# The down projection of a fp32 feed-forward layer, emitted in an explicit order per engine

## The chip, the cores and the metric

The kernel runs on one core of a Trainium2 chip. The metric is the device time of one execution in microseconds (us). A core has a matmul engine (TensorE, PE in the profile), a vector engine (VectorE, DVE), an activation engine (ScalarE, ACT), a general engine (GpSimd, POOL) and SyncE (SP), which here only issues DMAs. Each engine runs its own instruction queue in order and waits on semaphores for what others produce.

## The reference

One decoder layer over a sequence of 2048 tokens of width 1024: a mixer of three kinds of heads, then a gated feed-forward block with a short causal convolution. The change lies in the feed-forward block:

```python
def _conv_glu(h, w_up, conv_w, conv_b, w_down):
    u = _causal_dwconv(h @ w_up, conv_w) + conv_b
    gate, up = jnp.split(u, 2, axis=-1)
    return (jax.nn.silu(gate) * up) @ w_down
...
    x = x + _mixer(...)
    h = _rms(x, norm_ffn_g[l])
    x = x + _conv_glu(h, w_up[l], ffn_conv_w[l], ffn_conv_b[l], w_down[l])
```

Everything is float32. `w_up` is 1024 x 5632, `w_down` 2816 x 1024.

## The kernel before, in words

**Number format.** Matmul operands are split in two parts, a high part rounded to the fast fp32r format and the remainder `lo = x - h`. A product is the sum of three matmuls: high-high, high-low, low-high. So each operand tile costs a ScalarE copy (`h`) and a subtraction on VectorE or GpSimd (`lo`) before TensorE can read it.

**Halves.** The feed-forward block runs over the sequence in two halves (`hf` 0 and 1, 1024 tokens each): `ffn_up(0)`, `ffn_down(0)`, `ffn_up(1)`, `ffn_down(1)`. `ffn_up` writes the gated activations, in seven combinations, to the scratch tensor `s_g` in DRAM (lines L1112 and L1119, DMAs on ScalarE's queue), and `w_blocks` writes four combinations of blocks of `w_down` to `s_w`, in half 0 only.

**Down projection.** `ffn_down` multiplies 2 x 2 blocks by the Strassen-Winograd scheme: seven products instead of eight. A product (inner function `product`, matmuls at L1187) has `nj` = 11 steps j; a step takes one 128 x 512 tile of `s_g` (`g_parts`: load L1151 on SyncE's queue, copy L1152 on ScalarE, subtraction L1153 on VectorE) and one of the weights (`w_parts`: load L1160 from `s_w` or L1165 from `w_down`, copy L1166 on ScalarE, subtraction L1167 on GpSimd), and issues 3 matmuls for each of four 128 x 512 output tiles. The four output tiles of a product are two PSUM tiles of two banks; `ps_tile` rotates over four such places. The products run in the order of pairs (operand of `s_g`, operand of the weights) (0,4), (1,5), (5,1), (6,2), (3,3), (4,0), (2,6).

**Sums and stores.** After a product VectorE adds it into an accumulator (`u`, `v`; helper `tt`, L1205) or into the output. Four quarters of the output of a half leave: after products 2, 5, 6 and 7. For each, `base` loads the residual x2 (four tiles of tag `tmp`, four buffers, L1210, SyncE's queue) at step j = 4 of the product, and `store` adds and sends it out (L1218, DMA on ScalarE's queue). The first quarter's x2 is loaded straight into an accumulator (L1202). ScalarE copies the first product to `u` (L1224).

**Next half's operands.** `h_parts(k, 1, 0)` and `h_parts(k, 1, 1)` prepare the right operands of `ffn_up(1)` in half 0: at step 4 of the second and of the fourth product they emit, for four blocks dt one after the other, loads of `s_h` (L957), differences (VectorE, L962) and splits (`h_split`: ScalarE L944, VectorE or GpSimd L945). `up_blocks(k, k.hpool, 0, "a11 a12 a22")` at step 4 of the last product loads (L988) and splits (L993 on ScalarE, L994 on GpSimd) the first three weight blocks of `ffn_up(1)`.

**Buffers.** Operand tiles of the down projection come from one pool of 23 buffers of 128 x 512 (`fw`, tag `w`), which `ffn_up` also uses for its weight blocks; accumulators from 5 buffers (tag `u`), x2 tiles from 4 (tag `tmp`). `hpool` has 10 buffers. A tile's buffer is free once every reader of the previous tile in it is done.

**What sets the order.** The program is written with a framework whose planner simulates the engines and places each instruction in its engine's queue when its simulated inputs and buffers are ready, earlier emitted ones first. So the order of each queue around the down projection is the planner's: it may place loads, splits and sums of a product, the next half's operands and the up projection's matmuls (L1030) among each other. The queues then run in that order on the chip, each instruction waiting for its semaphores. All buffer waits and dependencies are put in by the framework.

Of the kernel before, what the change touches and what calls it, by code (L numbers as in the profile page):

```python
# [9 lines left out]
F32 = mybir.dt.float32  # L10
F32R = mybir.dt.float32r
# [3 lines left out]
AF = mybir.ActivationFunctionType  # L15
ALU = mybir.AluOpType
# [4 lines left out]
P = 128  # L21
# [8 lines left out]
NP = DFF // P  # L30
BLK = 512
# [9 lines left out]
RZ, RA = 2.5, 2  # L41

ZC = 6

ORDER = (
    "bo ci cg bv b0 b1 c0 c1 k0 k1 q0 q1 v0 v1",
# [895 lines left out]
def h_split(k, n, dt, x, eng):  # L942
    h, lo = k.hp[n]
    k.nc.scalar.activation(h[:, dt, :], x, AF.Copy)  # L944
    eng.tensor_tensor(lo[:, dt, :], x, h[:, dt, :].bitcast(F32), op=ALU.subtract)  # L945


def h_parts(k, hf, part):

    nc = k.nc  # L950
    for dt in range(4):
        def tmp():
            return k.t(k.hpool, [P, BLK], tag="w")

        def raw(q, s):
            t = tmp()
            nc.sync.dma_start(t, k.s_h[hf, q, s, :, dt, :])  # L957
            return t

        def sub(x, y):  # L960
            t = tmp()
            nc.vector.tensor_tensor(t, x, y, op=ALU.subtract)  # L962
            return t

        r12, r22 = raw(0, 1), raw(1, 1)
        if part == 0:
            r11, r21 = raw(0, 0), raw(1, 0)
            h_split(k, "b11", dt, r11, nc.gpsimd)
            t1 = sub(r12, r11)
            t2 = sub(r22, t1)  # L970
            h_split(k, "t1", dt, t1, nc.vector)
            h_split(k, "t2", dt, t2, nc.vector)
            h_split(k, "b21", dt, r21, nc.gpsimd)
            h_split(k, "t4", dt, sub(t2, r21), nc.vector)
        else:
            h_split(k, "t3", dt, sub(r22, r12), nc.vector)
            h_split(k, "b22", dt, r22, nc.gpsimd)


def up_blocks(k, fw, p, names):  # L980


    nc = k.nc

    def raw(q, ct):
        t = k.t(fw, [P, 4, P], tag="w")
        src = k.a["w_up"][0][q * BLK : (q + 1) * BLK, ct * P : (ct + 1) * P]
        nc.sync.dma_start(t, src.rearrange("(dt p) c -> p dt c", p=P))  # L988
        return t

    def parts(t):
        h, lo = (k.t(fw, [P, 4, P], F32R, tag="w") for _ in range(2))
        nc.scalar.activation(h, t, AF.Copy)  # L993
# [10 lines left out]
    if "s1" not in names:  # L1004
        for n, q, ct in (("a11", 0, p), ("a12", 1, p), ("a22", 1, NP + p)):
            if n in names:
                blocks[n] = parts(raw(q, ct))
        return blocks
# [92 lines left out]
def ps_tile(k, shape):  # L1101

    k.psp = k.psp[1:] + k.psp[:1]
    return k.t(k.psp[-1], shape, tag="ps")
# [31 lines left out]
def ffn_down(k, hf, fw):  # L1136

    nc = k.nc  # L1140
    first = {}
    x2_at = k.s_x2[hf * HALF : (hf + 1) * HALF].rearrange("(s i p) c -> p s i c", p=P, i=4)
    out_at = k.out[0, hf * HALF : (hf + 1) * HALF].rearrange("(s i p) c -> p s i c", p=P, i=4)

    def quarter(x, s, n):
        return x[:, s, :, n * BLK : (n + 1) * BLK]

    def g_parts(n, j):
        h, lo = (k.t(fw, [P, BLK], F32R, tag="w") for _ in range(2))
        raw = lo.bitcast(F32)  # L1150
        nc.sync.dma_start(raw, k.s_g[hf, n, j])  # L1151
        nc.scalar.activation(h, raw, AF.Copy)  # L1152
        nc.vector.tensor_tensor(lo, raw, h.bitcast(F32), op=ALU.subtract)  # L1153
        return h, lo

    def w_parts(n, j):
        h, lo = (k.t(fw, [P, BLK], F32R, tag="w") for _ in range(2))
        if n < 4:
            raw = lo.bitcast(F32)
            nc.sync.dma_start(raw, k.s_w[n, j])  # L1160
        else:
            raw = k.t(fw, [P, BLK], tag="w")
            q, c = ((0, 0), (1, 0), (1, 1))[n - 4]
            r = (q * (NP // 2) + j) * P
            nc.sync.dma_start(raw, k.a["w_down"][0][r : r + P, c * BLK : (c + 1) * BLK])  # L1165
        nc.scalar.activation(h, raw, AF.Copy)  # L1166
        nc.gpsimd.tensor_tensor(lo, raw, h.bitcast(F32), op=ALU.subtract)  # L1167
        return h, lo

    def product(na, nb, mid=None, last=False):  # L1170

        ps = [ps_tile(k, [P, 2, BLK]) for _ in range(2)]
        tiles = [ps[i // 2][:, i % 2, :] for i in range(4)]
        nj = NP // 2

        tail = 3 if last else 1
        parts = []
        for j in range(nj):
            parts.append((g_parts(na, j), w_parts(nb, j)))
            if mid is not None and j == 4:  # L1180
                mid()
            js = [j] if j < nj - tail else list(range(nj - tail, nj)) if j == nj - 1 else []
            for i in range(4):
                for m in js:
                    g, w = parts[m]
                    for c, (x, y) in enumerate(((0, 0), (0, 1), (1, 0))):
                        nc.tensor.matmul(  # L1187
                            tiles[i],
                            g[x][:, i * P : (i + 1) * P],
                            w[y],  # L1190
                            start=m == 0 and c == 0,
                            stop=m == nj - 1 and c == 2,
                        )
        return tiles

    def acc():
        t = [k.t(fw, [P, 2, BLK], tag="u", bufs=5) for _ in range(2)]
        return [t[i // 2][:, i % 2, :] for i in range(4)], t

    def load(t, s, n):  # L1200
        for i in range(2):
            nc.sync.dma_start(t[i], quarter(x2_at, s, n)[:, 2 * i : 2 * i + 2, :])  # L1202

    def tt(o, x, y, op=ALU.add):
        nc.vector.tensor_tensor(o, x, y, op=op)  # L1205

    def base(xs, s, n):
        for i in range(4):
            x = k.t(fw, [P, BLK], tag="tmp", bufs=4)
            nc.sync.dma_start(x, quarter(x2_at, s, n)[:, i, :])  # L1210
            xs.append(x)

    def store(xs, v, ps, s, n, op):

        for i in range(4):
            tt(ps[i], v[i], ps[i], op)
            tt(xs[i], xs[i], ps[i])
            nc.scalar.dma_start(quarter(out_at, s, n)[:, i, :], xs[i])  # L1218

    v, vt = acc()  # L1220
    p1 = product(0, 4, lambda: load(vt, 0, 0))
    u, _ = acc()
    for i in range(4):
        nc.scalar.activation(u[i], p1[i], AF.Copy)  # L1224
        tt(v[i], v[i], p1[i])
    p2 = product(1, 5, (lambda: h_parts(k, 1, 0)) if hf == 0 else None)
    for i in range(4):
        tt(v[i], v[i], p2[i])
    for i in range(2):
        nc.scalar.dma_start(quarter(out_at, 0, 0)[:, 2 * i : 2 * i + 2, :], vt[i])  # L1230
    p6 = product(5, 1)
    for i in range(4):
        tt(u[i], u[i], p6[i])
    p7 = product(6, 2, (lambda: h_parts(k, 1, 1)) if hf == 0 else None)
    v, _ = acc()
    for i in range(4):
        tt(v[i], u[i], p7[i])
    x4, x5, x3 = [], [], []
    p4 = product(3, 3, lambda: base(x4, 1, 0))
    store(x4, v, p4, 1, 0, ALU.subtract)  # L1240
    p5 = product(4, 0, lambda: base(x5, 1, 1))
    for i in range(4):
        tt(u[i], u[i], p5[i])
    store(x5, v, p5, 1, 1, ALU.add)

    def mid():
        base(x3, 0, 1)
        if hf == 0:
            first.update(up_blocks(k, k.hpool, 0, "a11 a12 a22"))

    p3 = product(2, 6, mid, last=hf == 1)
    store(x3, u, p3, 0, 1, ALU.add)
    return first


# [18 lines left out]
def _trunk(ctx, tc, a, out):  # L1274
    nc = tc.nc
    k = K(ctx, tc, a, out)
# [32 lines left out]
    with ExitStack() as ms:  # L1309
# [29 lines left out]
        with ExitStack() as at:  # L1339
# [14 lines left out]
            w = w_out_load(k, pool(wo, "wo", 1, side="right"), pool(wor, "wor", 1, side="right"))  # L1354
# [173 lines left out]
```

## Time and profile before

| | us |
|---|---|
| median of 3 runs | 3068.32 (3062.26 to 3069.09) |
| the profiled execution | 3064.58 |
| its span, first to last instruction | 3062.8 |
| mean granted TensorE clock | 0.965 of full |
| down projection, half 0: first to last matmul of L1187 | about 2120.8 to 2396.3 |
| down projection, half 1 | about 2823.1 to 3056.4 |

The profile comes from one execution. Its page lists busy times by engine, the span in 40 slices (busy tenths, granted clock, DMA), the DMA queues, the chain that ended last, and groups of instructions by source line with the idle time in front of them and what ended that. The trace behind it answers questions on single instructions, on waits (who waited for whom), and on stretches of time. In rows of the timeline a bracket `[idle before <-releaser]` tells how long the engine stood idle before the instruction and what released it; `x15` is the number of instructions merged into the row. PE is the matmul, PEld the weight load that goes with it; SPq and ACTq are instructions that only the queue of that engine carries, such as the issue of a DMA. A few per cent of the matmul records are missing.

### The profile page before, as it was taken

The numbers are of one execution on the slowest core, as the hardware profiler recorded it, in microseconds if no ns is written. First come the engines' busy times: TensorE is split into PE (matmuls) and PEld (weight loads), VectorE is DVE, ScalarE is ACT, GpSimd is POOL, SyncE is SP. The second block draws the span as 40 slices with busy tenths as digits, with TensorE's granted clock in tenths as the row PEclk, the third lists the DMA queues.
The fourth block names the chain that finished last, engine by engine and source line by source line (L and its number), as shares of the span: only waits on it lengthen the run. The fifth ranks groups of instructions, "written<-read, shape, count | busy, mean of one in ns | idle before, by whom it ended". The sixth has DMA issues, their size and how long they took to land. (4 is left out here: it accounts for less than half of the span.)

```text
span 3062.8 us, 43239 instructions
## 1 busy us (share of the span) xinstructions
PE 2867.9 (94%) x15181; PEld 2356.9 (77%) x15181; DVE 2029.6 (66%) x3637; ACT 1267.4 (41%) x2138; POOL 1419.4 (46%) x1149
## 2 busy tenths in 40 slices
PE   7999999899888988999999999999698999999998
PEld 7889999898765665666787788888487788888776
DVE  6427688757388877777546677776743677777534
ACT  3232432313144556776324444444442444444433
POOL 2133434633255656656202666665653544443533
PEclk9999999999988989999999999999799999999998
DMA  5333434423443034450356444546665333334654
GB/s 165 117 120 125 145 101 139 137 69 113 126 94 95 23 75 105 90 101 15 117 178 208 136 163 159 160 160 203 217 210 184 122 105 104 104 104 152 220 180 171
DMA packets 331897, 406.88 MB, mean 133 GB/s; under 512 B 30882, under 2 KB 219376, under 8 KB 328512
## 3 DMA queue, kind: packets, MB, share of 16 engines
q1 hardware_dynamic: 291520, 326.98, 35.8%
q10 hardware_dynamic: 37808, 68.76, 6.1%
q0 software_dynamic: 2352, 8.39, 1.0%
q8 instruction: 119, 1.95, 0.3%
q14 instruction: 98, 0.80, 0.1%
HBM read 276.05 MB, written 127.98 MB: 132 GB/s over the span
## 5 line engine op out<-in xcount | busy, mean ns | idle before, releaser
L994 POOL TENSOR_TENSOR w<-w,w 128x512 fp32r<-128x512 f32 x308 | 416.9, 1367 | 399.4 <-ACT w L993 291.4
L1187 PE MATMUL ps<-w,w 128*128 128x512 f32 x1848 | 453.5, 406 | 51.0 <-ACT w L1166 31.9
L1187 PEld LDWEIGHTS ps<-w,w 128*128 128x128 f32 x1848 | 358.1, 196 | 145.5 <-ACT w L1166 40.0
L164 PE MATMUL w<-whi,hhi 128*128 128x256 f32 (+1 forms) x1280 | 367.5, 288 | 2.3 <-DVE pg L226 1.7
L164 PE MATMUL w<-wlo,hhi 128*128 128x256 f32 (+1 forms) x1280 | 366.0, 287 | 0.6 <-POOL wlo L155 0.6
L164 PE MATMUL w<-whi,hlo 128*128 128x256 f32 (+1 forms) x1280 | 365.1, 286 | 0.0
L1167 POOL TENSOR_TENSOR w<-w,w 128x512 fp32r<-128x512 f32 x154 | 220.9, 1443 | 274.9 <-ACT w L1166 233.6
L781 POOL TENSOR_TENSOR pl<-pf,ph 128x512 fp32r<-128x512 f32 (+1 forms) x224 | 268.3, 1210 | 172.3 <-ACT ph L778 111.2
L993 ACT ACTIVATE w<-w 128x512 fp32r<-128x512 f32 x308 | 184.6, 628 | 273.3 <-POOL w L994 78.2
L1153 DVE TENSOR_TENSOR w<-w,w 128x512 fp32r<-128x512 f32 x154 | 158.2, 1048 | 147.9 <-ACT w L1152 142.7
L164 PEld LDWEIGHTS w<-whi,hhi 128*128 128x128 f32 x1280 | 244.0, 191 | 3.9 <-issue 2.2
L164 PEld LDWEIGHTS w<-wlo,hhi 128*128 128x128 f32 x1280 | 243.6, 191 | 1.8 <-POOL wlo L155 1.0
L164 PEld LDWEIGHTS w<-whi,hlo 128*128 128x128 f32 x1280 | 243.6, 191 | 0.2
L743 DVE TENSOR_REDUCE mx<-m 128x1 f32<-128x512 f32 (+2 forms) x320 | 188.6, 605 | 63.8 <-PE m L738 33.6
L776 ACT ACTIVATE pf<-s 128x512 f32<-128x512 f32 (+1 forms) x320 | 168.5, 539 | 140.2 <-DVE pl L781 49.3
L155 POOL TENSOR_TENSOR wlo<-wraw,whi 128x1024 fp32r<-128x1024 f32 (+1 forms) x56 | 137.8, 2481 | 171.9 <-ACT whi L154 169.0
L778 ACT ACTIVATE ph<-pf 128x512 fp32r<-128x512 f32 (+1 forms) x320 | 178.1, 575 | 46.1 <-PE pv L796 39.0
L999 DVE TENSOR_TENSOR w<-w,w 128x512 f32<-128x512 f32 x176 | 151.2, 878 | 69.1 <-DMA w<-in_w_up_dram 61.1
L1152 ACT ACTIVATE w<-w 128x512 fp32r<-128x512 f32 x154 | 97.0, 630 | 192.6 <-DMA w<-s_g 112.3
L1045 DVE SCALAR_TENSOR_TENSOR u<-ps,fcol,u 128x1023 f32<-128x1023 f32 x88 | 108.9, 1279 | 90.7 <-ACT u L1044 90.7
L769 PE MATMUL s<-QB,KB 70*128 70x512 f32 (+1 forms) x320 | 133.4, 417 | 29.3 <-ACT pf L776 29.0
L738 PE MATMUL m<-KB,QB 70*128 70x512 f32 (+2 forms) x320 | 135.3, 438 | 26.4 <-DVE mx L743 13.5
(345 smaller groups left out, 7087.6 us busy)
## 6 DMA issues: line engine op xcount, KB each, us to landing
w<-in_w_up_dram SPq DMA_DIRECT2D x182, 256.0 KB
w<-s_g SPq DMA_DIRECT2D x154, 256.0 KB
w<-in_w_down_dram SPq DMA_DIRECT2D x110, 256.0 KB
wraw<-in_w_in_dram SPq DMA_DIRECT2D x48, 512.0 KB
s_g<-u ACTq DMA_DIRECT2D x88, 256.0 KB
w<-s_w SPq DMA_DIRECT2D x88, 256.0 KB
s_g<-w ACTq DMA_DIRECT2D x66, 256.0 KB
w<-s_h SPq DMA_DIRECT2D x48, 256.0 KB
```

Of the source, the lines that this page charges most:

```text
L155: nc.gpsimd.tensor_tensor(lo[:, q : q + n, :], raw, h.bitcast(F32), op=ALU.subtract)
L164: nc.tensor.matmul(out, lsl(lhs[a], i), rsl(rhs[b], i), start=(i == 0 and j == 0), stop=(i == n - 1 and j == 2))
L743: nc.vector.tensor_reduce(mx[:, i, kb : kb + 1], ps[:, 0:n], axis=AX.X, op=ALU.max)
L776: nc.scalar.activation(pf[:, c0:], ps[:, c0:], AF.Exp)
L778: nc.scalar.activation(ph[:, c0:], pf[:, c0:], AF.Copy)
L781: eng.tensor_tensor(pl[:, c0:], pf[:, c0:], ph[:, c0:].bitcast(F32), op=ALU.subtract)
L993: nc.scalar.activation(h, t, AF.Copy)
L994: nc.gpsimd.tensor_tensor(lo, t, h.bitcast(F32), op=ALU.subtract)
L999: nc.vector.tensor_tensor(t, x, y, op=op)
L1153: nc.vector.tensor_tensor(lo, raw, h.bitcast(F32), op=ALU.subtract)
L1167: nc.gpsimd.tensor_tensor(lo, raw, h.bitcast(F32), op=ALU.subtract)
L1187: nc.tensor.matmul(tiles[i], g[x][:, i * P : (i + 1) * P], w[y], start=m == 0 and c == 0, stop=m == nj - 1 and c == 2,)
```

## The change

All of `ffn_down` is put in a region in which every engine keeps the order in which instructions are emitted (`manual_schedule`). Where the region's instructions fall among instructions outside it is still the planner's. The 7 x 11 = 77 steps are numbered through, and the loop emits for step i, in this order:

- the loads of step i + 4 (`AHEAD`);
- at j = 7 of the products 1, 5, 6, 7, the loads of the four x2 tiles (for the first product into `tmp` tiles too, not into an accumulator);
- at j = 1 to 4, the store of one output tile of the product before, on SyncE's queue instead of ScalarE's;
- in half 0, at steps 8, 15, ... 57, the loads of one of eight pieces of the next half's operands (`h_unit`), and at step 65 those of its first weight blocks (`up_first`); their splits follow five steps later;
- the splits of step i + 2;
- the matmuls of step i (in half 1 the last three steps of the last product tile by tile, as before);
- at j = 0 to 3, the sum of one output tile of the product before.

The matmuls, the number of VectorE sums, the bytes moved and the buffers are as before; 512 KB loads and stores of x2 and of the first quarter become 256 KB ones. `up_first` also serves the first half, ahead of `ffn_up(0)`; there it issues its three loads before its splits.

```diff
-def h_parts(k, hf, part):
-    nc = k.nc
-    for dt in range(4):
...
+def h_unit(k, hf, part, dt):
...
+    r12, r22 = raw(0, 1), raw(1, 1)
+    if part == 0:
+        r11, r21 = raw(0, 0), raw(1, 0)
+
+    def rest():
         if part == 0:
-            r11, r21 = raw(0, 0), raw(1, 0)
             h_split(k, "b11", dt, r11, nc.gpsimd)
             t1 = sub(r12, r11)
             t2 = sub(r22, t1)
...
+    return rest
+
+def up_first(k):
+    raws = {}
+    for n, q, ct in (("a11", 0, 0), ("a12", 1, 0), ("a22", 1, NP)):
+        t = raws[n] = k.t(k.hpool, [P, 4, P], tag="w")
...
+        nc.sync.dma_start(t, src.rearrange("(dt p) c -> p dt c", p=P))
+    def rest():
+        blocks = {}
+        for n, t in raws.items():
+            h, lo = blocks[n] = tuple(k.t(k.hpool, [P, 4, P], F32R, tag="w") for _ in range(2))
+            nc.scalar.activation(h, t, AF.Copy)
+            nc.gpsimd.tensor_tensor(lo, t, h.bitcast(F32), op=ALU.subtract)
+        return blocks
+    return rest
...
+    def loads(i):
+        n, j = steps[i]
+        raws[i] = load_g(prods[n][0], j), load_w(prods[n][1], j)
+
+    def parts(i):
+        (gr, gh, gl), (wr, wh, wl) = raws.pop(i)
+        nc.scalar.activation(gh, gr, AF.Copy)
+        nc.scalar.activation(wh, wr, AF.Copy)
+        nc.vector.tensor_tensor(gl, gr, gh.bitcast(F32), op=ALU.subtract)
+        nc.gpsimd.tensor_tensor(wl, wr, wh.bitcast(F32), op=ALU.subtract)
+        ready[i] = (gh, gl), (wh, wl)
...
+    def x2_tile(s, n, i):
+        t = k.t(fw, [P, BLK], tag="tmp", bufs=4)
+        nc.sync.dma_start(t, quarter(x2_at, s, n)[:, i, :])
+        return t
...
+    def sums(n, i, ps):
+        if n == 0:
+            nc.scalar.activation(st["u"][i], ps, AF.Copy)
+            tt(st["c"][i], st["u"][i], st["x"][i])
+        elif n == 1:
+            tt(st["x1"][i], st["c"][i], ps)
...
+        if n in (4, 5, 6):
+            x = st["x"][i]
+            tt(ps, st["u" if n == 6 else "v"][i], ps, ALU.subtract if n == 4 else ALU.add)
+            tt(x, x, ps)
+    def store(n, i):
+        if n in where:
+            nc.sync.dma_start(quarter(out_at, *where[n])[:, i, :], st["x1" if n == 1 else "x"][i])
+    side = {}
+    if hf == 0:
+        for m in range(8):
+            side[8 + 7 * m] = lambda m=m: h_unit(k, 1, m // 4, m % 4)
+        side[65] = lambda: up_first(k)
+    later = {}
+    tail = 3 if hf == 1 else 1
+    with k.tc.manual_schedule():
+        for i in range(AHEAD):
+            loads(i)
+        for i in range(2):
+            parts(i)
+        tiles = {}
+        for i, (n, j) in enumerate(steps):
+            if i + AHEAD < len(steps):
+                loads(i + AHEAD)
+            if j == 7 and n in (0, 4, 5, 6):
+                st["x"] = [x2_tile(*(where[n] if n else (0, 0)), t) for t in range(4)]
+            if n > 0 and 1 <= j <= 4:
+                store(n - 1, j - 1)
+            if i in side:
+                later[i + 5] = side[i]()
+            if i + 2 < len(steps):
+                parts(i + 2)
+            if i in later:
+                first = later.pop(i)() or first
+            if j == 0:
+                tiles[n] = quads([ps_tile(k, [P, 2, BLK]) for _ in range(2)])
...
+                for t in range(4):
+                    mm(tiles[n], i, t)
+            if n > 0 and j < 4:
...
+                sums(n - 1, j, tiles[n - 1][j])
+    for t in range(4):
+        sums(6, t, tiles[6][t])
+        store(6, t)
     return first
...
-    first = up_blocks(k, k.hpool, 0, "a11 a12 a22")
+    first = up_first(k)()
```

More of the change, by code (lines that the diff above doesn't have):

```diff
@@ L43 @@
 ZC = 6
+AHEAD = 4
 ORDER = (
@@ L945, in h_split, with tmp, raw, sub @@
     eng.tensor_tensor(lo[:, dt, :], x, h[:, dt, :].bitcast(F32), op=ALU.subtract)
-def h_parts(k, hf, part):
+def h_unit(k, hf, part, dt):
     nc = k.nc
-    for dt in range(4):
[L952 to L965, printed above, removed]
+    def tmp():
+        return k.t(k.hpool, [P, BLK], tag="w")
+    def raw(q, s):
+        t = tmp()
+        nc.sync.dma_start(t, k.s_h[hf, q, s, :, dt, :])
+        return t
+    def sub(x, y):
+        t = tmp()
+        nc.vector.tensor_tensor(t, x, y, op=ALU.subtract)
+        return t
+    r12, r22 = raw(0, 1), raw(1, 1)
+    if part == 0:
+        r11, r21 = raw(0, 0), raw(1, 0)
+    def rest():
         if part == 0:
-            r11, r21 = raw(0, 0), raw(1, 0)
             h_split(k, "b11", dt, r11, nc.gpsimd)
@@ L977, in h_parts @@
             h_split(k, "b22", dt, r22, nc.gpsimd)
+    return rest
+def h_parts(k, hf, part):
+    for dt in range(4):
+        h_unit(k, hf, part, dt)()
+def up_first(k):
+    nc = k.nc
+    raws = {}
+    for n, q, ct in (("a11", 0, 0), ("a12", 1, 0), ("a22", 1, NP)):
+        t = raws[n] = k.t(k.hpool, [P, 4, P], tag="w")
+        src = k.a["w_up"][0][q * BLK : (q + 1) * BLK, ct * P : (ct + 1) * P]
+        nc.sync.dma_start(t, src.rearrange("(dt p) c -> p dt c", p=P))
[7 more added lines that the diff above has]
+    return rest
 def up_blocks(k, fw, p, names):
@@ L1003, in up_blocks @@
     blocks = {}
[L1004 to L1008, printed above, removed]
     a11, a21, a22, a12 = raw(0, p), raw(0, NP + p), raw(1, NP + p), raw(1, p)
@@ L1146, in quarter, with load_g @@
         return x[:, s, :, n * BLK : (n + 1) * BLK]
-    def g_parts(n, j):
+    def load_g(n, j):
         h, lo = (k.t(fw, [P, BLK], F32R, tag="w") for _ in range(2))
@@ L1151, in g_parts, with load_w @@
         nc.sync.dma_start(raw, k.s_g[hf, n, j])
[L1152 to L1156, printed above, removed]
+        return raw, h, lo
+    def load_w(n, j):
         h, lo = (k.t(fw, [P, BLK], F32R, tag="w") for _ in range(2))
@@ L1163, in w_parts @@
             q, c = ((0, 0), (1, 0), (1, 1))[n - 4]
-            r = (q * (NP // 2) + j) * P
+            r = (q * nj + j) * P
             nc.sync.dma_start(raw, k.a["w_down"][0][r : r + P, c * BLK : (c + 1) * BLK])
[L1166 to L1194, printed above, removed]
@@ L1196, in acc @@
-    def acc():
[L1197 to L1202, printed above, removed]
+        return raw, h, lo
+    nj = NP // 2
+    prods = ((0, 4), (1, 5), (5, 1), (6, 2), (3, 3), (4, 0), (2, 6))
+    steps = [(n, j) for n in range(7) for j in range(nj)]
+    raws, ready = {}, {}
+    def loads(i):
+        n, j = steps[i]
+        raws[i] = load_g(prods[n][0], j), load_w(prods[n][1], j)
@@ new lines, in parts, with mm @@
+    def parts(i):
[5 more added lines that the diff above has]
+        ready[i] = (gh, gl), (wh, wl)
+    def mm(tiles, i, tile):
+        n, j = steps[i]
+        g, w = ready[i]
+        for c, (x, y) in enumerate(((0, 0), (0, 1), (1, 0))):
+            nc.tensor.matmul(
+                tiles[tile],
+                g[x][:, tile * P : (tile + 1) * P],
+                w[y],
+                start=j == 0 and c == 0,
+                stop=j == nj - 1 and c == 2,
+            )
@@ L1204, in tt, with quads @@
+    def quads(t):
+        return [t[i // 2][:, i % 2, :] for i in range(4)]
+    def acc():
+        return quads([k.t(fw, [P, 2, BLK], tag="u", bufs=5) for _ in range(2)])
+    def x2_tile(s, n, i):
+        t = k.t(fw, [P, BLK], tag="tmp", bufs=4)
+        nc.sync.dma_start(t, quarter(x2_at, s, n)[:, i, :])
+        return t
     def tt(o, x, y, op=ALU.add):
         nc.vector.tensor_tensor(o, x, y, op=op)
[L1207 to L1252, printed above, removed]
+    st = {}
+    where = {1: (0, 0), 4: (1, 0), 5: (1, 1), 6: (0, 1)}
+    def sums(n, i, ps):
[4 more added lines that the diff above has]
+            tt(st["x1"][i], st["c"][i], ps)
+        elif n == 2:
+            tt(st["u"][i], st["u"][i], ps)
+        elif n == 3:
+            tt(st["v"][i], st["u"][i], ps)
+        elif n == 5:
+            tt(st["u"][i], st["u"][i], ps)
+        if n in (4, 5, 6):
+            x = st["x"][i]
+            tt(ps, st["u" if n == 6 else "v"][i], ps, ALU.subtract if n == 4 else ALU.add)
+            tt(x, x, ps)
@@ new lines, in store @@
+    def store(n, i):
[29 more added lines that the diff above has]
+                tiles[n] = quads([ps_tile(k, [P, 2, BLK]) for _ in range(2)])
+            if n == 6 and j >= nj - tail:
+                if j == nj - 1:
+                    for t in range(4):
+                        for m in range(i - tail + 1, i + 1):
+                            mm(tiles[n], m, t)
+            else:
+                for t in range(4):
+                    mm(tiles[n], i, t)
+            if n > 0 and j < 4:
+                if j == 0 and n == 1:
+                    st["u"], st["c"] = acc(), acc()
+                if j == 0 and n == 2:
+                    st["x1"] = [k.t(fw, [P, BLK], tag="tmp", bufs=4) for _ in range(4)]
+                if j == 0 and n == 4:
+                    st["v"] = acc()
+                sums(n - 1, j, tiles[n - 1][j])
@@ L1253, in ffn_down @@
+    for t in range(4):
+        sums(6, t, tiles[6][t])
+        store(6, t)
     return first
```

## The prediction

> **What bounds the kernel now.** I read the page first: engine shares and clock line, then the groups, then the same lines by stretches of time.
>
> ```profile
> PE 2867.9 (94%) x15181; PEld 2356.9 (77%) x15181; DVE 2029.6 (66%) x3637; ACT 1267.4 (41%) x2138; POOL 1419.4 (46%) x1149
> PEclk9999999999988989999999999999799999999998
> L1187 PE MATMUL ps<-w,w 128*128 128x512 f32 x1848 | 453.5, 406 | 51.0 <-ACT w L1166 31.9
> ```
>
> TensorE (PE) is the bound nearly everywhere, and the one slice in which its granted clock falls to 7 tenths lies in the changed function, `ffn_down`, whose matmuls are line L1187. The third row says that PE stood idle for 51.0 us in front of them. A stretch in which PE is never idle shows what those matmuls cost when fed:
>
> ```profile
> L1187 PE MATMUL ps<-w,w x1848: 387/389/796, 2120.8 to 3056.0; 128*128 128x512 f32 x185
> 2122.65 3.56 PE L1187 MATMUL ps<-w,w 128*128 128x512 f32 x15
> 2920.00:2965.00 45.00, 45.00 (x200) 37.13 (x199) 17.41 (x22) 21.08 (x34) 21.38 (x18) 1.00 0.60 192
> ```
>
> A matmul lasts 0.39 us (the least and the median of the first row, 387 and 389 ns), overlapping the next; fifteen in a row take 3.56, so the pitch is (3.56 - 0.39)/14 = 0.2264 us. A step of a product is 4 tiles x 3 matmuls = 12, or 2.72 us; a half (7 products x 11 steps) is 924 matmuls or 209.2 us. The third row, a window (columns: PE, PE's weight loads, VectorE, ScalarE, GpSimd busy, clock, DMA share, GB/s) shows that the present buffers, transfers and engines can feed PE without a gap. Against the 209.2 us stand the stretches of L1187 alone, both halves:
>
> ```profile
> 2120.83:2128.31 7.48, 7.48 (x33) 6.01 (x32) 1.00 0.68 225
> 2133.75:2202.00 68.25, 45.90 (x143) 31.60 (x143) 0.77 0.72 245
> 2202.00:2364.39 162.39, 151.80 (x641) 122.10 (x640) 0.97 0.56 188
> 2369.83:2396.28 26.45, 25.20 (x108) 19.93 (x107) 1.00 0.68 215
> 2823.10:3056.40 233.30, 216.47 (x897) 172.69 (x896) 0.96 0.59 196
> ```
>
> The first four are half 0 (the two gaps of 5.44 us between them, 24 matmuls each, are the up projection's). Length less count x 0.2264 gives what is lost: 0.0, 35.9, 17.3 and 2.0 us, together 55.2. The fifth is half 1: 233.3 - 209.2 = 24.1 us (27 of its 924 records are missing, so the full count is used). So **79.3 us** of PE time can be had in the two down projections, and nothing else that the diff touches holds as much. PE's waits account for part, the lowered clock after them for the rest:
>
> ```profile
> PE ps L1187 <- ACT w L1166: 12.0, 6, 4.5
> PE ps L1187 <- POOL w L1167: 4.5, 7, 0.7
> 2154.76 1.22 PE L1187 MATMUL ps<-w,w 128*128 128x512 f32 x2 [5.25 <-ACT w L1166]
> 2841.03 0.73 PE L1187 MATMUL ps<-w,w 128*128 128x512 f32 x2 [2.13 <-ACT w L1166]
> 2842.39 3.96 PE L1187 MATMUL ps<-w,w 128*128 128x512 f32 x10 [0.63 <-POOL w L1167]
> 2986.64 3.85 PE L1187 MATMUL ps<-w,w 128*128 128x512 f32 x7 [4.46 <-ACT w L1166]
> ```
>
> In half 1 the waits are 16.5 us, and 24.1 - 16.5 = 7.6 is clock: two matmuls take 1.22 us behind the wait of 5.25, 0.73 behind the one of 2.13. Both must go together.
>
> **Where the waits come from.** The chain of waits back from the one at 2986.64:
>
> ```profile
> 2974.70 0.35 ACTq L1218 DMA_DIRECT2D out_dram<-tmp  x1
> 2975.18 0.63 ACT L1152 ACTIVATE w<-w 128x512 fp32r<-128x512 f32 x1 [10.50 <-DVE tmp L1205]
> SPq L1210 <- DMA out_dram<-tmp: 34.3, 8, 12.7
> 2983.35 0.32 SPq L1210 DMA_DIRECT2D tmp<-s_x  x1
> 2985.96 0.63 ACT L1166 ACTIVATE w<-w 128x512 fp32r<-128x512 f32 x1 [3.69 <-DMA w<-s_w]
> ```
>
> Two queues are blocked in order. ScalarE's holds a store (L1218) that waits for VectorE's sum, and the operand copy L1152 behind it stood 10.50 us. SyncE's holds the x2 loads of the next product (L1210), which need one of the four `tmp` buffers and so wait for those stores to land (34.3 us in half 1, up to 12.7 at once); all operand loads stand behind them, and the first weight operand loaded afterwards reaches L1166 at 2985.96, 0.7 us ahead of PE. Half 0 has the same two jams (the 17.3 us) and, in the stretch with 35.9, the whole of the next half's operands: `h_parts` for four blocks at once, in the middle of the second product.
>
> **The change part by part.**
>
> *x2 loads and stores.* The loads move from the step j = 4 of the product that uses them, placed by the planner, to j = 7; each store goes out one step behind its sum, at j = 1 to 4, from SyncE's queue. So at j = 7 the store issued at j = 4 has had 3 x 2.72 = 8.2 us. What a transfer of this size needs is seen where nothing queues:
>
> ```profile
> 3042.58 0.32 SPq L1151 DMA_DIRECT2D w<-s_g  x1
> 3043.00 0.37 SPq L1165 DMA_DIRECT2D w<-in_w_down_dram  x1
> 3045.18 0.63 ACT L1152 ACTIVATE w<-w 128x512 fp32r<-128x512 f32 x1 [1.44 <-DMA w<-s_g]
> 3045.91 0.63 ACT L1166 ACTIVATE w<-w 128x512 fp32r<-128x512 f32 x1
> 3046.62 1.29 POOL L1167 TENSOR_TENSOR w<-w,w 128x512 fp32r<-128x512 f32 x1 [1.51 <-ACT w L1166]
> ```
>
> 2.60 us from issue to use for a load; a store, which no row here times better, I put at 3. Both waits fall away: the 17.3 us of half 0 and the part of half 1's 24.1 that is not the 2.8 of its start (below). ScalarE loses its store issues (0.35 each), SyncE gains them: at most 2 loads, 1 store and 4 tiles of h in one step, 7 x 0.37 = 2.6 us, in a queue that needs 0.7 in the ordinary step. What now stands behind a store on SyncE is the next operand load; the store waits for a sum that VectorE does about 2 us after the step before began, and SyncE arrives there only when PE has finished that step. Cost nil. If that cover went, each store could hold the loads by under a step, against a lead of more than four.
>
> *The lead.* Loads are bound by 23 `w` buffers, before and after: four for each step, five where w_down comes raw. The load rows of half 1 run from 2800.62; 41 of them stand up to 2922.44, 21 up to 2869.58:
>
> ```profile
> 2800.62 0.33 SPq L1151 DMA_DIRECT2D w<-s_g  x1
> 2869.58 0.32 SPq L1151 DMA_DIRECT2D w<-s_g  x1
> 2922.44 0.32 SPq L1151 DMA_DIRECT2D w<-s_g  x1
> 2823.10:2869.58 46.48, 42.93 (x177) 33.89 (x177) 0.96 0.69 234
> 2823.10:2922.44 99.34, 95.11 (x406) 76.52 (x406) 0.98 0.68 224
> ```
>
> By busy time PE is then in step 42.93/2.72 = 15.8 and 35.0, so step 20 and step 40 are loaded 4.2 and 5.0 steps ahead. The diff's four ahead is what the buffers give already: no gain, no loss. From the issue at 3042.58 to the end of L1167 at 3047.91 are 5.3 us; 4.2 steps are 11.4, so 6.1 us are spare.
>
> *Sums.* The same 44 VectorE operations a half (0.69 each), one tile a step. A sum waits for a product that has just ended and delays the split two steps ahead by up to 3 x 0.69 = 2.1 us, inside the spare 6.1. PSUM holds two products, as before. Cost nil.
>
> *Next half's operands.* Eight pieces, one every 7 steps, loaded five steps before they are split. The rows of one piece before:
>
> ```profile
> L945 DVE TENSOR_TENSOR t1l<-w,t1h 128x512 fp32r<-128x512 f32 x4 | 7.1, 1773 | 0.0
> L945 DVE TENSOR_TENSOR t2l<-w,t2h 128x512 fp32r<-128x512 f32 x4 | 2.7, 679 | 0.0
> 2175.42 1.71 POOL L945 TENSOR_TENSOR b11l<-w,b11h 128x512 fp32r<-128x512 f32 x1 [1.16 <-ACT b11h L944]
> 2175.93 1.74 DVE L1153 TENSOR_TENSOR w<-w,w 128x512 fp32r<-128x512 f32 x1
> ```
>
> A piece of part 0 is 5 ScalarE copies (3.2 us), 6 VectorE subtractions and 2 on GpSimd. VectorE's take 0.68 alone but 1.7 beside a GpSimd one: the row at 2175.93 ends at 2177.67, 0.54 after GpSimd's. If the two exclude each other, a piece adds 6 x 0.68 + 2 x 1.29 = 6.7 us, and 7 steps of splits need 7 x (0.68 + 1.29) = 13.8: 20.5 against 7 x 2.72 = 19.0, that is 1.5 us late a piece, 6.0 for four. If they only slow each other, the piece's chain of 6.7 us is nearly the spare 6.1, and the cost is near 0. I take the former, 6.0, since the rows of that stretch are nearest to it. The Trainium skill's GPSIMD Engine Reference (Specifications) has the same as a rule, GpSimd's memory interface being shared with VectorE where that reads two SBUF inputs; it speaks against this part, and by it the sum is the one that I take, without it 6.0 us less. Pieces of part 1 (2 VectorE, 1 GpSimd: 2.7 us) fit in the 5.2 that 7 steps leave, and `up_first` (3 on GpSimd, 3.9 us) too. Upper bound: half of the present 35.9, 18 us, if bursts of one block hurt half as much as four in a row.
>
> *Start of each half.* The wait at 2841.03 with its 0.63 behind it falls into the tail of the up projection's work on ScalarE and VectorE, which the diff leaves alone: 2.8 us stay in each half, 5.6 (0 to 10).
>
> *End.* The 2.0 us of half 0's last stretch I leave in both halves: 4.0. Behind half 0 stands the way into the next up projection:
>
> ```profile
> 2397.11 0.34 ACTq L1218 DMA_DIRECT2D out_dram<-tmp  x1
> 2399.05 0.79 PE L1030 MATMUL ps<-t2h,w 128*128 128x512 f32 x1 [2.77 <-ACT w L993]
> 2400.11 0.60 ACT L1068 ACTIVATE tmp<-ps 128x512 f32<-128x512 f32 x1 [0.59 <-DMA out_dram<-tmp]
> 2400.76 0.80 PE L1030 MATMUL ps<-b21h,w 128*128 128x512 f32 x1 [0.49 <-ACT tmp L1068]
> ```
>
> The 24 up matmuls that ran at 2364, inside a jam, can now fill this gap (2.77 + 0.49, and some 2 of slow clock, 0.80 a matmul for 0.39: a gain of up to 5.3); or the stores, now in the queue of the up projection's loads, delay it as much. I take 0.
>
> **Sum:** -79.3 + 6.0 + 5.6 + 4.0 = -63.7 us. The profiled execution took 3064.58 (span 3062.8), so 3000.9; the median of the runs is 3.7 above it, so 3004.6, say 3005.
>
> **Rivals.** *The pieces don't fit*: a late piece lets the lead drain, the next finds it shorter, and half 0 keeps 18 us plus some 7 of clock: 79.3 - 25 - 9.6 = 45 gained or less, 3022 to 3035. For it: the stretch at 0.77 clock; against: the pieces now lie 19 us apart. *The way between the stages also gains*: 5.3 more, and both starts clean: about 2994. *Slower*: strict order cuts the lead. A step's buffers are claimed in one order on every engine, and if that leaves 2 steps between load and use, 5.44 us, against a path of 5.3 plus some 0.7 of queueing at two loads a step, each of 154 steps loses 0.56 us: 86 us, more than the 79.3, hence 3075. It decides below 2.2 steps; against it stand the 4.2 and 5.0 above with the same buffers. *It does nothing*: the planner still places the up projection's work between, and new jams of the old size arise at other products: 3062 to 3074.
>
> **How the numbers follow.** The forecast (2995 to 3021) 0.68, the larger gain 0.08, the pieces 0.13, nothing 0.04, slower 0.07. The range of 2984 to 3030 leaves out nothing and slower and the end of the pieces. Two kernels are told apart at about 0.2%, 6 us: faster 0.89, same 0.04, slower 0.07.
>
> **What would show it.** In the profile after: the wait of x2 loads for stores gone from SyncE's queue; ScalarE no longer idle 10 us on a sum; half 1's stretch of down matmuls near 214 us at clock 1.0, half 0's near 220, its waits in groups 19 us apart behind the split of part 0; a first wait of 2 to 3 us early in each half. Wrong it would be if waits come at every step, if the pieces' waits exceed 3.4 us in sum each, or if the up stages (L1030) move by more than 6 us.

## The result, and the profile after

The changed kernel takes **2983.26 us** (median of 4 runs, 2981.18 to 2985.5), the kernel before, on the same chip, 3065.29 (4 runs, 3060.76 to 3069.09): a ratio of 0.9733 (95% interval 0.9715 to 0.9751), a gain of 82 us. The forecast was 3005 with a range down to 2984: the sign was right, some 20 us of the gain were missing in it, and the time lies 0.7 us under the range. The profiled execution took 2985.5 us, its span 2983.7.

From the page of the changed kernel: engine shares, the clock line, and the group of the down projection's matmuls (now line L1215):

```profile
PE 2837.8 (95%) x15181; PEld 2347.6 (79%) x15181; DVE 2054.4 (69%) x3637; ACT 1256.0 (42%) x2138; POOL 1413.7 (47%) x1149
PEclk9999999999987998999999999999999999999999
L1215 PE MATMUL ps<-w,w 128*128 128x512 f32 x1848 | 422.5, 390 | 4.0 <-ACT w L1206 2.0
```

The idle time in front of these matmuls fell from 51.0 to 4.0 us, and no slice after the middle of the span has a lowered clock. PE's busy time fell by 30 us for the same 15181 matmuls: a matmul lasts longer at the lower clock that had followed the waits. By stretches (columns as before), L1215 alone:

```profile
2123.81:2132.93 9.12, 8.09 (x34) 6.19 (x34) 1.00 0.63 203
2138.36:2345.73 207.37, 204.31 (x890) 167.79 (x889) 0.99 0.77 260
2762.56:2769.59 7.03, 7.03 (x31) 5.63 (x30) 1.00 0.62 193
2775.03:2977.60 202.57, 202.57 (x893) 167.42 (x892) 1.00 0.67 225
```

The gap of 5.4 us in each half holds 24 matmuls of the up projection. Half 0 lasts 2345.89 - 2123.81 = 222.1 us for 948 matmuls, which need 214.6 at 0.2264; half 1 lasts 215.0 us for the same 948. Done for all four stages, in both kernels, with the interleaved matmuls counted where they ran, this gives the PE time lost:

| stage | its matmuls | lost before, us | lost after, us |
|---|---|---|---|
| up projection, half 0 | 1848 | 13.5 | 16.9 |
| down projection, half 0 | 924 | 55.4 | 7 |
| up projection, half 1 | 1848 | 7.6 | 4.0 |
| down projection, half 1 | 924 | 30.4 | 0.3 |

The differences sum to 78.7; the spans differ by 79.1. So the whole gain lies in the two down projections (48.4 and 30.1), and the up stages balance.

The waits behind it, half 0. First ScalarE's in front of the operand copies before (three lines: for loads, for a sum), then after:

```profile
ACT w L1152 <- DMA w<-s_g: 50.5, 31, 7.7
ACT w L1166 <- DMA w<-in_w_down_dram: 11.8, 9, 5.0
ACT w L1152 <- DVE tmp L1205: 12.9, 2, 10.6
```

```profile
ACT w L1206 <- PE ps L1215: 20.8, 16, 2.0
ACT w L1205 <- POOL w L1208: 16.7, 12, 2.2
```

Before, the copies waited for operands to land, and for a sum behind a blocked store. Now they wait for buffers that PE and GpSimd give back: the supply is ahead of TensorE. SyncE's queue, half 0, after:

```profile
SPq L1179 <- PE ps L1215: 63.3, 39, 2.8
SPq L1260 <- DVE tmp L1235: 27.8, 14, 5.8
```

The x2 loads (now L1231) no longer wait for stores. The stores (L1260), on SyncE now, wait 27.8 us for sums, and nothing of it reaches PE. All that PE still waited in half 0:

```profile
2126.45 6.64 PE L1215 MATMUL ps<-w,w 128*128 128x512 f32 x28 [1.03 <-ACT halo L1076]
2176.34 0.50 PE L1215 MATMUL ps<-w,w 128*128 128x512 f32 x1 [1.95 <-ACT w L1206]
2177.89 22.43 PE L1215 MATMUL ps<-w,w 128*128 128x512 f32 x90 [1.04 <-POOL w L1208]
```

One piece of the next half's operands (the one split at 2166 to 2176) shows, three do not, and half 1 has no wait at all.

### The profile page after: what moved, and what is told of

It reads as the page before. It is cut to its first block, busy times and chain, and to the rows that moved or that the text cites. A ratio compares the mean times of both kernels' runs of the same rounds, so it can differ in the third digit from the quotient of the medians.

```text
span 2983.7 us, 43125 instructions
## 1 busy us (share of the span) xinstructions
PE 2837.8 (95%) x15181; PEld 2347.6 (79%) x15181; DVE 2054.4 (69%) x3637; ACT 1256.0 (42%) x2138; POOL 1413.7 (47%) x1149
## 3 DMA queue, kind: packets, MB, share of 16 engines
q8 instruction: 119, 1.95, 0.3%
## 5 line engine op out<-in xcount | busy, mean ns | idle before, releaser
L1027 POOL TENSOR_TENSOR w<-w,w 128x512 fp32r<-128x512 f32 x302 | 405.2, 1354 | 401.4 <-ACT w L1026 342.0
L1215 PE MATMUL ps<-w,w 128*128 128x512 f32 x1848 | 422.5, 390 | 4.0 <-ACT w L1206 2.0
L1215 PEld LDWEIGHTS ps<-w,w 128*128 128x128 f32 x1848 | 347.6, 188 | 78.1 <-ACT w L1206 2.4
L1208 POOL TENSOR_TENSOR w<-w,w 128x512 fp32r<-128x512 f32 x154 | 215.9, 1409 | 203.2 <-ACT w L1206 159.6
L1207 DVE TENSOR_TENSOR w<-w,w 128x512 fp32r<-128x512 f32 x154 | 179.0, 1171 | 106.8 <-ACT w L1205 103.6
L740 PE MATMUL m<-KB,QB 70*128 70x512 f32 (+2 forms) x320 | 137.1, 443 | 27.4 <-DVE mx L745 14.0
```

The costliest lines, as they stand in the source:

```text
L1207: nc.vector.tensor_tensor(gl, gr, gh.bitcast(F32), op=ALU.subtract)
L1208: nc.gpsimd.tensor_tensor(wl, wr, wh.bitcast(F32), op=ALU.subtract)
L1215: nc.tensor.matmul(tiles[tile], g[x][:, tile * P : (tile + 1) * P], w[y], start=j == 0 and c == 0, stop=j == nj - 1 and c == 2,)
```

## The experiments

The changed kernel alters several things at once: the fixed order, the lookahead, the places of x2 loads and stores, the spread sums, the pieces. Theory A is the prediction's: the gain comes from the new places of x2 loads and stores (no jam) and from the pieces. Its first rivals were that the fixed order itself does it (B) or that the stores' move to SyncE's queue does (C). Differences of under some 6 us between kernels are not told apart here unless the trace tells them.

**1. The same code, the planner's order.**

```diff
-    with k.tc.manual_schedule():
+    with ExitStack():
```

> The changed kernel with the same emission order, but without the region that fixes it: the planner places every instruction again. Theory A (the gain is where x2 loads, stores and the next half's pieces stand in the queues): the planner pulls the pieces and x2 loads forward as soon as its simulated buffers are free, so some of the jams return: 3000 to 3040 us, with x2 loads waiting on SyncE for stores. Theory B (the gain is the fixed order as such, that the planner's simulated times never fit the chip): about 3060. Theory C (the stores' move from ScalarE's to SyncE's queue did it): about 2983, unchanged.

2989.84 us (2987.67 to 2992.74), ratio 0.9754 (0.974 to 0.9769). That is 6.6 us more than the changed kernel, and the intervals of the two ratios overlap: little or nothing is due to the fixed order, and B falls. The order of emission does the rest, with the planner free to undo it. A, with 3000 to 3040, was too slow; C's 2983 was nearest, and run 5 tests it alone. A had not asked *which* of the new emission places the planner follows.

**2. The jam put back.** Loads two ahead; for products 6 and 7 x2 loaded right behind the stores, in a burst, stores on ScalarE.

```diff
-AHEAD = 4
+AHEAD = 2
...
+                elif j == 0:
+                    for t in range(4):
+                        sums(n - 1, t, tiles[n - 1][t])
+                        nc.scalar.dma_start(quarter(out_at, *where[n - 1])[:, t, :], st["x"][t])
+                    st["x"] = [x2_tile(*where[n], t) for t in range(4)]
```

> The changed kernel, order still fixed, with the jam put back at products 6 and 7: the four sums of the product before are emitted together at j = 0, its four stores right behind them on ScalarE's queue, and the x2 loads of the next tile behind those, ahead of the loads of step 3 (loads two steps ahead instead of four, to reach that place). Theory A: SyncE runs some five steps ahead of TensorE and stops at the x2 loads until the stores have landed; two jams in each half with clock loss, as before: 25 to 40 us slower than the changed kernel, 3008 to 3023. Theory B: within 5 us of it, 2980 to 2990. Theory C: half of its gain lost, above 3020.

**3. The next half's operands in two bursts.**

```diff
-        for m in range(8):
-            side[8 + 7 * m] = lambda m=m: h_unit(k, 1, m // 4, m % 4)
+        side[15] = lambda: h_parts(k, 1, 0)
+        side[37] = lambda: h_parts(k, 1, 1)
```

> The changed kernel, order still fixed, with the next half's operands in two bursts again: the four blocks of part 0 loaded and split at step 15, those of part 1 at step 37. Theory A: half 0's down matmuls lose 25 to 36 us round step 15 and little at step 37 (2.7 us of work a block instead of 6.7): 3008 to 3020. Theory B: within 5 us of the changed kernel, 2980 to 2990.

**4. Loads two steps ahead.** `AHEAD = 2` alone.

> The changed kernel with loads emitted two steps ahead instead of four. Theory A: how far the loads run ahead is set by the 23 buffers, not by the emission, as SyncE waits for nothing else: within 5 us of the changed kernel, 2980 to 2988. Rival (the four steps ahead are what feeds TensorE): two steps are 5.4 us against a path of 5.3 and more from a load's issue to its use, 0.3 to 0.6 us lost in each of 154 steps: 3030 to 3075.

Run 2 took 3034.84 us (0.9898, 0.9878 to 0.9917), run 3 3019.86 (0.9852, 0.9836 to 0.9869), run 4 2999.17 (0.979, 0.9774 to 0.9806). From the traces, run 2 (SyncE's wait of half 0 and two of PE's waits), then run 3, then run 4:

```profile
SPq L1231 <- DMA out_dram<-tmp: 30.1, 8, 10.1
2301.45 0.79 PE L1215 MATMUL ps<-w,w 128*128 128x512 f32 x1 [6.14 <-ACT w L1206]
2342.44 0.80 PE L1215 MATMUL ps<-w,w 128*128 128x512 f32 x1 [8.11 <-ACT w L1206]
```

```profile
2199.21 0.80 PE L1215 MATMUL ps<-w,w 128*128 128x512 f32 x1 [24.10 <-ACT w L1206]
2269.13 0.79 PE L1215 MATMUL ps<-w,w 128*128 128x512 f32 x1 [6.31 <-ACT w L1206]
```

```profile
SPq L1260 <- DVE tmp L1235: 48.4, 15, 12.6
ACT w L1205 <- DMA w<-s_g: 62.7, 28, 4.8
2220.27 0.80 PE L1215 MATMUL ps<-w,w 128*128 128x512 f32 x1 [3.41 <-ACT w L1206]
```

Against run 4, with the same lead, run 2 costs 36 us, with four waits of 6 to 8 us behind x2 loads that stood for stores: the jam is real and of about the size that the prediction gave it (expected were 25 to 40 us against the changed kernel; against that it is 52, since the shorter lead costs too). Against the changed kernel run 3 costs 37 us, nearly all of it in two waits and the slow clock behind them. So with a fixed order both bursts are dear. Run 4 fits neither side: two steps less lead cost 16 us. The stores then stand two steps nearer the front of SyncE's queue and wait 48.4 us for sums, with the operand loads behind them (not behind the longest wait, 12.6: that is the first store of the last product, and no operand load of this half stands behind it). Counted load by load in half 0 from step 10 on, the loads behind the stores are issued as little as 1.5 steps ahead of TensorE, in the changed kernel never less than 3.5, and ScalarE's copies wait 62.7 us for loads of `s_g` (second row; 7.6 in the changed kernel). The wait of 3.41 us is one where such late loads meet a piece of the next half's operands, which held ScalarE for 2.84 us just before. How far loads run ahead thus decides where everything else stands in that queue; what a short lead alone costs, without stores in the way, no run separates.

**5. Stores back on ScalarE's queue, at their new steps. 6. `up_first` at the program's start written as before. 7. The pieces three steps later** (`side[11 + 7 * m]`).

> The changed kernel with the stores of the output on ScalarE's queue instead of SyncE's, at the same places of the emission, order fixed. Theory A: a store on ScalarE waits at most for the sum of the step before, inside the spare time of the splits: 2980 to 2990. Theory C (the stores' move is where the gain comes from): half of it lost or more, above 3020.

> The changed kernel with the first three weight blocks of the up projection's first half loaded and split one by one, as before the change. Theory A: the 3 us that the first up stage has become longer (waits of TensorE on the splits at its start, 2.1 instead of 0.3 us, and later ones) come from that order: 2979 to 2982, the first up stage at its old length. Rival: they come from the planner's other placements, and nothing moves: 2982 to 2985.

> The changed kernel with all eight pieces of the next half's operands three steps later (loads at steps 11, 18, ..., splits at 16, 23, ...), so that the first of part 0 no longer falls together with the sums of the first product, which use ScalarE and two memory operands on VectorE. Theory A: the only wait of half 0's steady stretch (1.95 and 1.04 us, and the slow clock behind it) goes: 2977 to 2981. Rival (a piece of part 0 exceeds the spare time wherever it stands): the wait moves with it, 2982 to 2986.

They took 2989.41 us (0.9755, 0.9732 to 0.9778), 2986.86 (0.9745, 0.9728 to 0.9762) and 2982.96 (0.9739, 0.9715 to 0.9763). None is told apart from the changed kernel. The queue of the stores decides little as long as they go out one by one, and C falls. The up stage of half 0 lost 17.0, 17.4 and 15.3 us in them, so the 3.4 that it lost more after the change is not the doing of `up_first`. It need not be the change's at all: all twelve runs lie between 15.3 and 17.6, and run 9, whose code of this stage is that of before, lost 16.4. Shifted pieces shift the wait, from the first piece of part 0 to the third:

```profile
2219.91 0.50 PE L1215 MATMUL ps<-w,w 128*128 128x512 f32 x1 [2.52 <-ACT w L1206]
```

**8. The planner, and no lookahead.** Each step's loads and splits emitted with its matmuls; spread sums, late x2 loads, pieces and stores on SyncE as in the changed kernel. By now there was a theory D: the planner places x2 loads and operands in SyncE's queue by its own simulated times. When loads are emitted ahead, its SyncE runs ahead, and what must wait for a store comes to stand behind more operand loads.

> The kernel of e1 (order left to the planner) with each step's loads and splits emitted with its matmuls, no steps ahead; stores stay on SyncE, x2 loads and pieces at the same emission steps. Theory D, formed on e1: what moves the planner is that loads and splits are emitted ahead, as it then lets SyncE run ahead in its simulation too and puts x2 loads and pieces behind more loads; without that it puts the x2 loads of the second half of the products some five steps and the pieces up to fifteen steps nearer to the front, as in the kernel before, and the jams return: 3035 to 3065. Rival (sums and stores spread over steps, or the stores' queue, did it in e1): 2985 to 3000.

3040.51 us (3032.97 to 3047.71), 0.9924 (0.9893 to 0.9954). Everything but the lookahead and the fixed order brings 23 us of the 82; half 0 lost 41.4 and half 1 15.9 us. Waits of the kind of before are back:

```profile
2159.53 1.22 PE L1215 MATMUL ps<-w,w 128*128 128x512 f32 x2 [3.96 <-ACT w L1206]
2203.46 11.92 PE L1215 MATMUL ps<-w,w 128*128 128x512 f32 x44 [3.29 <-POOL w L1208]
```

**9. The kernel before, with x2 loads and pieces emitted late.**

```diff
-    p5 = product(4, 0, lambda: base(x5, 1, 1))
+    p5 = product(4, 0, lambda: base(x5, 1, 1), at=9, side=pieces(5))
...
-    p2 = product(1, 5, (lambda: h_parts(k, 1, 0)) if hf == 0 else None)
+    p2 = product(1, 5, side=pieces(1))
```

> The kernel before, with the x2 loads emitted at step 9 (7 in the last product) instead of 4, and the next half's operands emitted in eight pieces seven steps apart instead of two bursts; the planner keeps the order. Theory D (the planner places the transfers in SyncE's queue by its own times, so the place at which they are emitted in the code decides nothing): no change, 3055 to 3072 us, the waits of x2 loads for stores stay above 20 us a half. Rival (the later place in the code is what removes the jams): 3000 to 3020 us.

**10. The planner, and the lookahead alone.**

```diff
-    with k.tc.manual_schedule():
+    with ExitStack():
...
-            if j == 7 and n in (0, 4, 5, 6):
+            if j == 4 and n in (0, 4, 5, 6):
...
-                sums(n - 1, j, tiles[n - 1][j])
+                if j == 0:
+                    for t in range(4):
+                        sums(n - 1, t, tiles[n - 1][t])
+                        store(n - 1, t)
```

with stores on ScalarE and the operands in two bursts.

> The planner orders, and of the change only the lookahead is left: loads emitted four steps ahead, splits two. Sums and stores come in a burst behind each product, stores on ScalarE, x2 loads emitted at step 4, the next half's operands in two bursts, all as before. Theory D (with the loads emitted ahead, the planner puts the x2 loads behind more operand loads, and most of the jams go): 2985 to 3005 us, little lost in half 1. Rival (the jams need the spread sums, the later x2 loads and the pieces as well): 3030 to 3065 us.

Run 9: 3066.37 us, ratio 0.9997 (0.9981 to 1.0013). Run 10: 2993.82 (2992.37 to 2994.71), 0.9768 (0.9744 to 0.9791). This is the answer. The later places in the code, in which the prediction had put the gain, do nothing by themselves; the lookahead alone, with x2 at j = 4, sums and stores in bursts and operands in two bursts, brings 72 of the 82 us. SyncE's wait of x2 loads for stores in half 0, in run 9 and then in run 10, and the largest wait of PE left in run 10:

```profile
SPq L1224 <- DMA out_dram<-tmp: 34.3, 7, 12.8
```

```profile
SPq L1231 <- DMA out_dram<-tmp: 10.8, 10, 2.1
2171.14 18.93 PE L1215 MATMUL ps<-w,w 128*128 128x512 f32 x70 [4.99 <-DVE w L1207]
```

Run 10 is not quite the lookahead alone: it keeps the change's 256 KB transfers of the first quarter and `up_first`, and it has loads and splits ahead together. Which of the two leads does how much, no run separates.

Counted along SyncE's instructions in half 0, the number of `s_g` loads ahead of the x2 loads of products 6 and 7 and of the first and the last piece of operands:

| kernel | x2, product 6 | x2, product 7 | operands | x2 waits for stores, longest, us |
|---|---|---|---|---|
| before; run 9 | 57 to 58 | 69 to 70 | 9 to 14 | 12.8 |
| run 2 (jam) | 58 | 69 | 11 to 60 | 10.1 |
| run 8 (no lookahead) | 58 to 60 | 69 to 71 | 10 to 18 | 2.2 |
| run 10 (lookahead alone) | 63 to 65 | 74 to 76 | 13 to 33 | 2.1 |
| changed kernel | 67 | 77 | 13 to 62 | none |

Product 6 is steps 55 to 65. Before the change SyncE comes to this place 4.9 steps ahead of PE; behind 58 loads it meets the x2 loads while PE is in product 5, whose sums and stores must come first, and all operands behind them stand: the next load is issued only 1.0 step ahead. In run 10 SyncE is up to 5.9 steps ahead, and behind 63 to 65 loads it meets them when the stores are leaving. Run 8 has the old places; there the stores stand on SyncE in front of the x2 loads and wait for sums in their place (46.6 us in half 0). The late emission of run 9 is pulled to the very same places as before.

**11. Each part-0 piece in two halves, two steps apart. 12. Loads six ahead** (`AHEAD = 6`).

> The changed kernel with each piece of part 0 split in two, the second half two steps behind the first. Theory A (the remaining waits of half 0 behind the piece at 2176 come from one piece's work on VectorE and GpSimd in one go): they go, half 0 loses 1 to 4 us in place of 7, 2976 to 2981 us. Rival (they come from the order of loads on SyncE, whatever the size of a piece): no change, 2981 to 2986 us.

> The changed kernel with the loads six steps ahead instead of four. Theory A (the lead matters as the place of stores and x2 loads in SyncE's queue: further back they wait less for sums): the waits of stores on SyncE fall below the present 19 us in half 0, and the time is 2978 to 2986 us. Rival (23 buffers hold no six steps: the queue of SyncE stands at a buffer, and stores and x2 loads behind it come late): over 2990 us.

Run 11: 2986.22 us (2975.47 to 2990.19), 0.9737 (0.9714 to 0.9759). The waits behind the piece shrank to one (first row below; matmuls are L1222 there) and half 0 lost 5 us in place of 7, part of the way to the 1 to 4 of A, but the runs do not tell it from the changed kernel. Run 12: 2992.15 (2986.95 to 2994.04), 0.9758 (0.9737 to 0.978): the rival's side in time, but not by its mechanism, since the loads do run further ahead with the same 23 buffers (6.9 steps in the median, 5.9 in the changed kernel). All four part-0 pieces now show in PE (the other two rows are two of them), and the stores' wait on SyncE is unchanged, 27.4 us against 27.8 (the 19 of the expectation is too low). Six ahead is not better than four; that it is worse is not settled, since the intervals of the two ratios overlap.

```profile
2181.77 150.81 PE L1222 MATMUL ps<-w,w 128*128 128x512 f32 x660 [0.93 <-POOL w L1215]
```

```profile
2199.18 20.93 PE L1215 MATMUL ps<-w,w 128*128 128x512 f32 x84 [0.93 <-POOL w L1208]
2241.16 95.86 PE L1215 MATMUL ps<-w,w 128*128 128x512 f32 x420 [0.84 <-POOL w L1208]
```

No version beats the changed kernel by more than a measurement can tell.

## Why the prediction was right in sign and short in size

**Right.** The bound (PE starved in the down projections), the method (length less count times 0.2264 us), the two jams and the burst, and that waits and slow clock go together. Half 0's own 55.2 was read to within the 55.4 of the table. Runs 2 and 3 show that jam and burst cost about what was said.

**The sum, term by term.** Forecast in the profile: -63.7; measured: -79.1. The 15.4 between them:

- *The loss of half 1, 24.1, was 30.4.* The prediction took 897 records in the stretch from 2823.10 and called the other 27 missing. They were not: 28 matmuls of L1187 had run before 2823.10, amid the end of the up projection, as a window that starts earlier shows in the trace of before:

```profile
2740.00:2823.10 83.10, 6.28 (x28) 5.26 (x28) 1.00 0.37 119
```

  The needed time of the stretch was 28 x 0.2264 = 6.3 us less than the 209.2 set against it. The half 0 stretches had been counted by their records and were right. No record of these matmuls is missing, other than the introduction has it: each half has its 924. Of the 30.4 the waits are 16.5 and the slow clock 13.9, not 7.6.
- *Starts 5.6 and ends 4.0: nearly all gone.* Half 1 lost 0.3 in all after the change, half 0 showed only the 1.03 at 2126.45 ahead of its first piece. The step "the diff leaves that alone" failed: the wait at the start is one for operands, and these now come ahead. Run 10 has the 0.4 of half 1 with the lookahead alone.
- *Pieces 6.0.* That a part-0 piece can delay the splits behind it holds: the wait goes over to another piece in run 7 and shrinks when the pieces are halved in run 11. But the lead absorbs three of four. The Trainium skill's GPSIMD Engine Reference (Specifications) has GpSimd's SBUF interface shared with VectorE and names contention with instructions of two SBUF inputs, not that one excludes the other. How much of a piece's delay is this contention and how much the mere amount of work, no run here separates. Half 0 lost 7 us in all, of which the 1.95 and 1.04 are the piece's own waits. Starts, ends and pieces together were put at 15.6 and came to 7.3, or 8.3 us more gained.
- *The way into the next up projection, 0 taken of up to 5.3:* 3.6 gained (7.6 to 4.0). Against it the up stage of half 0, not priced, lost 3.4 more, which run 9 shows without the change too.

6.3 + 8.3 + 3.6 - 3.4 = 14.8, and 0.6 is rounding of the readings. So what came is nearest to the rival *the way between the stages also gains* (2994, a chance of 0.08), on top of a sum that was 6 us short.

**The step that failed in the mechanism.** "The diff's four ahead is what the buffers give already: no gain, no loss." The two rows that the prediction read lie between the jams. Counted at every load from step 10 on, the loads of the kernel before are issued 4.8 steps ahead in the median of each half, but about 1 step ahead behind the x2 loads; in the changed kernel it is 5.9 and never less than 3.5, in run 10 5.8 to 5.9 and never less than 3.7, in run 12 6.9. All of them have the same 23 buffers, so the buffers alone do not set the lead; by what way they allow more of it now stays open. And the place in the code at which loads are emitted decides where the planner puts everything else among them in SyncE's queue. The prediction gave the gain to the moved x2 loads, the spread sums and the pieces; run 9 shows that two of these without the lookahead bring nothing, run 8 that all of them bring 23 us, run 10 that the lookahead without them brings 72. The prediction read right what would vanish, and credited the wrong edit for it. It also put the stores on SyncE at nil: true at four steps of lead (27.8 us of waits, none of PE's), and most likely not at two, where run 4 lost 16 us.

**Rivals.** *Slower, by a cut lead:* no sign of it at four ahead, and even two cost 16 us, not 86. *The pieces don't fit:* no. *It does nothing:* no.

**What would show it.** ScalarE's 10 us behind a sum and SyncE's x2 waits went, as said. Half 1 was to last 214 and lasts 209.6 without the up projection's 24 matmuls, half 0 216.6 against 220. Waits 19 us apart at four pieces: one came. A first wait of 2 to 3 us in each half: none.

## What to carry to other kernels

Where a planner orders the queues, ask of an edit what it does to the planner's places, not only what the edited lines do: a lookahead in the code that the buffers seem to give already moved 72 us. By the counts it did so above all by putting transfers that wait for something late behind more of those that wait for nothing. A queue that issues in order is read by position: count how many operand loads stand ahead of a transfer that has to wait, and compare with how far that queue runs ahead of the consumer. And when loss is taken as length less needed work, count the work in the same stretch, to its first instruction: records called missing had only run earlier.

## What was not expected of the hardware

How little the clock's price of a wait depends on its length. Here are the longest wait of the changed kernel's half 0 once more, one of run 2 and one of run 3, each with the row behind it:

```profile
2176.34 0.50 PE L1215 MATMUL ps<-w,w 128*128 128x512 f32 x1 [1.95 <-ACT w L1206]
2177.89 22.43 PE L1215 MATMUL ps<-w,w 128*128 128x512 f32 x90 [1.04 <-POOL w L1208]
2301.45 0.79 PE L1215 MATMUL ps<-w,w 128*128 128x512 f32 x1 [6.14 <-ACT w L1206]
2302.79 31.54 PE L1215 MATMUL ps<-w,w 128*128 128x512 f32 x131 [0.56 <-POOL w L1208]
2199.21 0.80 PE L1215 MATMUL ps<-w,w 128*128 128x512 f32 x1 [24.10 <-ACT w L1206]
2200.63 62.20 PE L1215 MATMUL ps<-w,w 128*128 128x512 f32 x263 [0.62 <-POOL w L1208]
```

From the first matmul to the end of the second row, less the second wait and less what fed matmuls need (0.2264 each, 0.39 for the last), 2.2 us are lost behind the wait of 1.95, 2.3 behind the one of 6.14 and 3.1 behind the one of 24.10. The granted clock is 0.50 for some us behind the short wait as behind the longer one (changed kernel, then run 2; matmuls, weight loads, clock):

```profile
2178.50:2181.50 3.00, 3.00 (x9) 2.35 (x8) 0.50 0.69 218
2302.79:2306.00 3.21, 3.21 (x8) 2.53 (x9) 0.50 1.02 373
```

So here many small waits are dearer than one jam of about the same sum: in the stretch 2133.75 to 2202.00 of the kernel before, PE is idle for 22.4 us in many pieces and loses 13.5 more to the clock, against 24.10 and 3.1 in run 3. The length of the first matmul behind a wait, 0.50 or 0.79, does not tell the price. The Trainium skill's page TensorE: Matmul & The Clock Gate (Part 1) has half the clock after an idle window of some 3.4 us. Read as the least length of a wait, that does not hold here: half the clock came after waits of 1.95 and 1.04 us with one matmul between, and in the kernel before the first matmul took 0.79 after a wait of 2.77 (at 2399.05).

Waits of an in-order queue are free in bulk as long as nothing behind them is late: SyncE stood 63.3 us for buffers and 27.8 for sums in half 0 after the change, and PE waited 4.0 us in both halves.
